# Two thirds of layer 1's modulation: from layer 0's attention to layer 1's scans

## The chip, the cores and the metric

The kernel runs on one core of one Trainium2 chip. The metric is the time of one execution on the device in microseconds (us), a median over several runs. One core has five engines that run side by side, each through its own list of instructions in order: TensorE (PE; its weight loads are shown apart as PEld), VectorE (DVE), ScalarE (ACT), GpSimd (POOL) and SyncE (SP), which here only issues the transfers between HBM and the core's memory.

## What is computed

A two-layer backbone with 512 latent and 256 context tokens of width 1024. Each layer has three mixers beside each other (RWKV-7 scans in both directions, latent attention, Hyena long convolutions), one output projection over all three, and a large feed-forward part (FFN) that picks experts. Each layer's normalisations and residual gates are set by a *modulation*, which depends on the conditioning vectors alone:

```python
mod_l = (jax.nn.silu(c) @ mod_w[li] + mod_b[li])[:, None, :]
mod_c = (jax.nn.silu(c_ctx) @ mod_w[li] + mod_b[li])[None, None, :]
shm_l, scm_l, gm_l, shf_l, scf_l, gf_l = jnp.split(mod_l, N_MOD, axis=-1)
p_l = (rms_norm(x, mix_norm[li]) * (1.0 + scm_l) + shm_l) @ w_in[li]
# ... rw_l, ml_l, hy_l: the three mixers on p_l ...
x = x + gm_l * (jnp.concatenate([rw_l, ml_l, hy_l], axis=-1) @ w_out[li])
x = x + gf_l * peer_ffn(rms_norm(x, ffn_norm[li]) * (1.0 + scf_l) + shf_l, ...)
```

`mod_w[li]` is a matrix of 1024 x 6144 in float32. Its first two sixths (`shm`, `scm`) are wanted at the layer's start, the third (`gm`) at the output projection, the fourth and fifth (`shf`, `scf`) at the FFN's norm, the last (`gf`) at the FFN's end.

## The kernel before

**The modulation.** `mods(li, ...)` computes one layer's modulation in 12 groups of 512 columns (two groups to a sixth). A group is 8 chunks of 128 rows. For a chunk SP loads a tile `w` of 256 KB (L400), ACT copies it to a rounded tile `wh` (L403), DVE, or POOL for every fourth chunk, forms the rest `wl = w - wh` (L404), and PE multiplies both with four columns of the conditioning (`silr`), two matmuls of 4x512 outputs into one PSUM tile. Behind the 8 chunks ACT copies the 4x512 sums to `row` (L408), four small matmuls with `sel` turn them, and DVE adds the bias into `modc` (L412). PSUM tiles have tags; the tag `ch`, with two buffers, is used both by these groups and by the steps of the RWKV scans (`rwkv_chain`).

**Who runs when.** The program is recorded once. `weave` takes tracks (generators) and always records the next piece of the track whose counter is lowest; a piece adds the number that it yields, which `scaled` multiplies. A track can also wait for marks (`after`). So the order on each engine is fixed by these numbers, and each engine then works through its own list.

In layer 0 the tracks are the scans, `hyenas()` (the convolutions), `attention()` and a statistic. When the scans are done, `hyenas()` goes on with `mods(1, ...)`, all 12 groups of layer 1, with 5 buffers of `w` and 3 of `wh` and `wl` (`MB = (5, 3)`) and a scale of 3.5 (`MS`). At that time `attention()` is in the latents' attention `mla(0, 1)`: per head the projection and rotation of q and k, the scores' maxima (`mx`, `top`), and a loop over blocks of keys (`tr<-qT,kTl`, the exponential `PT` on ACT L1225, `mm<-PT,Vl`), then a reciprocal (`rc`, L1231) and `zl` (L1233). The output projection `mixed(0, 1)` follows: per m one column block of the weights, 24 matmuls, the residual `row` (L762) and its squares, and at the end the norm for the FFN (`rsqrt` on DVE, a transposition at L623).

In layer 1, `scan()` does the scans over the latents, six steps of preparation and four chained sub-steps each (`rwkv_chain`: `R`, `U`, `S`), then the readout `rwkv_read` (`Y`, `zl` at L1102). `hyenas()` ends with the latents' convolution `hyena(1, 1)`, and `attention()` with `mla(1, 1)`. Nothing else is in the weave; then all pools but the layer's are closed and `mixed(1, 1)` and `ffn(1)` are recorded. The loads of `w_out` (L658) and of the residual rows (L593) come from SP's one queue.

Of the kernel before, what the change touches and what calls it, by code (L numbers as in the profile page):

```python
# [10 lines left out]
F32 = mybir.dt.float32  # L11
# [148 lines left out]
NL, NS = 12, 0.1  # L160
MB, CS, MX = (5, 3), 20, 0
FH = ()
MS, OX = 3.5, (2, 1)
HP, HC, HT = 300, 300, 300


# [78 lines left out]
class K:  # L245
# [137 lines left out]
        self.sel = sp.tile([4, 2], F32, name="sel")  # L383
        nc.vector.tensor_tensor(self.sel, self.ident[0:4, 0:2], self.ident[0:4, 2:4], op=OP.add)

    def mods(self, li, side, bufs, hb, es):

        nc, io = self.nc, self.io
        m = self.modc[li] = self.keep.tile([128, 48, 2], F32, name=f"modc{li}")
        sc = self.nrm[li] = self.keep.tile([128, 2, 8, 2], F32, name=f"sc{li}")  # L390
        mp, mw = [es.enter_context(self.pool(n, k, side=side)) for n, k in (("modp", 1), ("modw", 4))]
        b = mp.tile([128, 48], F32, name="b")
        nc.sync.dma_start(b, io["mod_b"][li])
        nr = mp.tile([128, 2, 8], F32, name="nr")
        nc.sync.dma_start(nr, io["norms"][li])
        for g in range(12):
            p = self.ps("ch")
            for k in range(8):
                w = mw.tile([128, 512], F32, name="w", bufs=bufs)
                nc.sync.dma_start(w, io["mod_w"][li, 128 * k:128 * k + 128, g * 512:(g + 1) * 512])  # L400
                wh = mw.tile([128, 512], F32R, name="wh", bufs=hb)
                wl = mw.tile([128, 512], F32R, name="wl", bufs=hb)
                nc.scalar.activation(wh, w, AF.Copy)  # L403
                (nc.gpsimd if k % 4 == 3 else nc.vector).tensor_tensor(wl, w, wh.bitcast(F32), op=OP.subtract)  # L404
                self.mm(p[0:4], self.sil[:, k], wh, k == 0, False)
                self.mm(p[0:4], self.sil[:, k], wl, False, k == 7)
            row = mp.tile([4, 512], F32, name="row", bufs=2)
            nc.scalar.activation(row, p[0:4], AF.Copy)  # L408
            p = self.ps("ch")
            for k in range(4):  # L410
                self.mm(p[:, 2 * k:2 * k + 2], row[:, k * 128:(k + 1) * 128], self.sel)
            nc.vector.tensor_tensor(m[:, 4 * g:4 * g + 4], p[:, 0:8].rearrange("p (m b) -> p m b", b=2),  # L412
                                    b[:, 4 * g:4 * g + 4, None].to_broadcast([128, 4, 2]), op=OP.add)
            if g in (3, 9):
                f = g // 6
                q = 8 * (3 * f + 1)
                nc.vector.scalar_tensor_tensor(sc[:, f], m[:, q:q + 8, :], 1.0,
                                               nr[:, f, :, None].to_broadcast([128, 8, 2]), op0=OP.add, op1=OP.mult)
            self.mark(("mod", li, g))
            yield 4  # L420
# [63 lines left out]
    def layer0(self):  # L484
        with ExitStack() as lay, ExitStack() as es:
# [17 lines left out]
            def hyenas():  # L503
                yield from self.hyena_filters(0, 0, "left")
                yield from self.hyena(0, 0, zc, "left")
                yield self.after(*FH)
                yield from self.hyena_filters(0, 1, "left")
                yield self.after("xc")
                yield from self.hyena(0, 1, zl, "left")
                yield self.after(("rwkv", 0, 1))  # L510
                es.close()
                yield from self.scaled(self.mods(1, "left", *MB, fin), MS)

            def attention():
                yield from self.mla(0, 0, [zc[:, m] for m in range(17, 21)], ymc, "right")
# [24 lines left out]
    def layer1(self):  # L540
        if self.done:
            return
        with ExitStack() as lay, ExitStack() as es:
            zl = self.open_layer(1, lay, 2)
            zkv = self.lp.tile([128, 2, TC], F32, name="zkv")
            yml = [zl[:, 11], zl[:, 15], zl[:, 12]]
            ctx = ExitStack()
            z = {}

            def scan():  # L550
# [7 lines left out]
            def hyenas():  # L558
                yield from self.hyena_filters(1, 1, "left")
                self.mark("flt")  # L560
                yield self.after("rw1")
                yield from self.hyena(1, 1, zl, "left")

            def attention():
                self.wcut = 4
                yield from self.project(1, 1, [(m, zl[:, m]) for m in ORDER], "right", self.h1)
                self.wcut = 8
                self.scale_par()
                self.mark("pl1")
                yield self.after("xc1", "flt")  # L570
                self.open_rwkv(es)
                zc = z["c"] = ctx.enter_context(self.pool("zc")).tile([128, 7, TC], F32, name="zc")
                self.rwk = [ctx.enter_context(self.pool(n, k)) for n, k in (("rwk", 1), ("rwp", 2))]
                self.mark("rwc")
                yield from self.project(1, 0, [(m, zc[:, m - 3] if m < 10 else zkv[:, m - 19]) for m in ORDER if m in (3, 4, 5, 6, 7, 8, 9, 19, 20)], "right")
                yield from self.mla(1, 0, [None, None, zkv[:, 0], zkv[:, 1]], None, "right")
                yield from self.mla(1, 1, [zl[:, m] for m in range(17, 21)], yml, "right")

            self.weave((0, self.context_out()), (0, attention()), (0, scan()), (0, self.scaled(hyenas(), HL1)))
            es.close()  # L580
            self.open_late(1)
            self.flat(self.mixed(1, 1, [zl[:, 0], zl[:, 1], zl[:, 2], *yml, zl[:, 13], zl[:, 14]], "left"))
# [1220 lines left out]
```

## Time and profile before

| what | us |
|---|---|
| median of 3 runs | 5449.75 |
| lowest, highest | 5433.88, 5454.05 |
| the profiled execution's own time | 5464.84 |
| its span on the core | 5463.1 |
| PE busy within it | 4928.4 |
| DVE busy within it | 3849.6 |

The profiled execution is one run; its span is what the trace covers, and its own time is 1.7 us longer. Busy times of PE come from recorded matmuls, which overlap their neighbours: a matmul of 512 columns is shown with 0.39 us and the next one starts 0.23 us later when the granted clock is 1.00. "Idle before, releaser" in a row names the wait of that engine just ahead of an instruction and what ended it. The layer-1 modulation lies at 998 to 1269 us, layer 1's convolution, scans and latent attention at about 3550 to 4061 us, and layer 1's output projection from 4061 to 4118 us.

### The profile page before, as it was taken

To read this page: it belongs to the slowest core of one execution; us is meant where nothing else is said; L and a number is where in the kernel's file an instruction comes from. 1 tells how busy PE (TensorE), PEld (TensorE's weight loads), DVE (VectorE), ACT (ScalarE), POOL (GpSimd) and SP (SyncE) were. 2 spreads that over 40 slices of the span, in tenths; PEclk is the share of its full clock that TensorE was granted. 3 is DMA by queue.
4 is the path that set the end of the run, shared out by engine and by line. 5 is a ranking of instruction groups with operands and counts; after the bars stand their busy time and mean duration, and the time that the engine had idled before them with its cause. 6 is when DMAs were issued, how large, how long until landed. Compare 5 with 4: busy or idle time off the path is not lost. (4 is left out here: it accounts for less than half of the span.)

```text
span 5463.1 us, 76042 instructions
## 1 busy us (share of the span) xinstructions
PE 4928.4 (90%) x28693; PEld 3745.5 (69%) x28693; DVE 3849.6 (70%) x8277; ACT 1918.5 (35%) x3438; POOL 1241.3 (23%) x933
## 2 busy tenths in 40 slices
PE   7987998889989999999999678888889889999998
PEld 4765676547644588887878456656657667888887
DVE  6356666656896488887888875656646985777776
ACT  5322222443254333333333232222223454444442
POOL 2322212221200122222222363211122321111110
PEclk9977899899999999999999889777899999999999
DMA  6300121342365788888888764200022668888885
GB/s 207 103 22 31 51 86 55 113 151 71 109 187 162 240 326 316 330 323 311 318 325 303 274 238 153 77 1 1 1 74 82 196 191 295 324 322 312 321 320 206
DMA packets 395517, 1028.18 MB, mean 188 GB/s; under 512 B 31780, under 2 KB 198981, under 8 KB 339597
## 3 DMA queue, kind: packets, MB, share of 16 engines
q1 hardware_dynamic: 339852, 620.65, 34.0%
q0 software_dynamic: 55296, 402.68, 19.6%
q8 instruction: 225, 3.69, 0.3%
q14 instruction: 144, 1.17, 0.1%
HBM read 920.19 MB, written 103.02 MB: 187 GB/s over the span
## 5 line engine op out<-in xcount | busy, mean ns | idle before, releaser
L203 POOL DMA_INDIRECT row<-in_uv,idx x384 | 531.8, 1385 | 1860.8 <-DVE acc L241 1586.7
L659 ACT ACTIVATE wh<-w 128x1024 fp32r<-128x1024 f32 (+1 forms) x557 | 571.0, 1027 | 1049.5 <-PE mm L272 461.7
L272 PE MATMUL mm<-hlo,wh 128*128 128x512 f32 (+2 forms) x2408 | 877.0, 368 | 30.7 <-DVE zl L688 7.5
L272 PE MATMUL mm<-hhi,wh 128*128 128x512 f32 (+2 forms) x2408 | 866.8, 364 | 0.0
L660 DVE TENSOR_TENSOR wl<-w,wh 128x1024 fp32r<-128x1024 f32 x424 | 516.3, 1221 | 255.0 <-ACT wh L659 252.1
L272 PE MATMUL mm<-hhi,wl 128*128 128x512 f32 (+2 forms) x2408 | 531.5, 361 | 1.7 <-POOL wl L660 1.7
L272 PEld LDWEIGHTS mm<-hlo,wh 128*128 128x128 f32 x2408 | 461.2, 192 | 104.4 <-issue 18.4
L241 DVE SCALAR_TENSOR_TENSOR acc<-row,act,acc 128x1024 f32<-128x1024 f32 x381 | 496.5, 1303 | 35.3 <-ACT act L237 34.6
L272 PEld LDWEIGHTS mm<-hhi,wh 128*128 128x128 f32 x2408 | 461.5, 192 | 61.8 <-issue 3.3
L219 DVE SCALAR_TENSOR_TENSOR row<-row,xk 128x1024 f32<-128x1024 f32 x384 | 480.3, 1251 | 16.5 <-DMA row<-in_uv,idx 16.3
L272 PE MATMUL mm<-row,wh 128*128 128x512 f32 (+1 forms) x1056 | 455.5, 574 | 29.9 <-DMA wh<-in_uT 25.1
L272 PEld LDWEIGHTS mm<-hhi,wl 128*128 128x128 f32 x2408 | 425.9, 189 | 56.6 <-issue 3.8
L660 POOL TENSOR_TENSOR wl<-w,wh 128x1024 fp32r<-128x1024 f32 (+1 forms) x133 | 291.4, 2198 | 670.0 <-ACT wh L659 405.3
L272 PEld LDWEIGHTS mm<-row,wh 128*128 128x128 f32 x1056 | 195.3, 195 | 211.2 <-issue 165.4
L236 ACT ACTIVATE act<-act 128x1 f32<-128x1 f32 x384 | 75.7, 197 | 498.6 <-DVE row L219 498.3
L1779 ACT ACTIVATE stage<-ch 128x512 f32<-128x512 f32 x224 | 218.2, 1101 | 62.6 <-PE ch L272 59.8
L1546 ACT ACTIVATE g<-mm 128x512 f32<-128x512 f32 (+1 forms) x256 | 137.6, 538 | 232.3 <-PE mm L272 197.2
L272 PE MATMUL rw<-wh,cl 128*128 128x512 f32 x512 | 201.5, 394 | 6.5 <-DVE cl L1614 3.5
L272 PE MATMUL rw<-wl,ch 128*128 128x512 f32 x512 | 200.5, 392 | 0.0
L272 PE MATMUL rw<-wh,ch 128*128 128x512 f32 x512 | 199.9, 390 | 0.0
L272 PE MATMUL ch<-wh,cl 128*128 128x512 f32 x512 | 199.6, 390 | 0.0
L272 PE MATMUL ch<-wh,ch 128*128 128x512 f32 x512 | 199.4, 389 | 0.0
(542 smaller groups left out, 10206.0 us busy)
## 6 DMA issues: line engine op xcount, KB each, us to landing
w<-in_uv SPq DMA_DIRECT2D x256, 512.0 KB
w<-in_uT SPq DMA_DIRECT2D x190, 512.0 KB
Wd<-stage SPq DMA_DIRECT2D x28, 2048.0 KB
w<-in_mod_w SPq DMA_DIRECT2D x192, 256.0 KB
wh<-in_uT SPq DMA_DIRECT2D x66, 512.0 KB
W<-Wd SPq DMA_DIRECT2D x32, 1024.0 KB
W<-Wd SPq DMA_DIRECT2D x32, 768.0 KB
w<-in_wq SPq DMA_DIRECT2D x32, 512.0 KB
```

The costliest lines, as they stand in the source:

```text
L203: self.nc.gpsimd.indirect_dma_start(out=row, out_offset=None, in_=self.k.io[f"uv{self.li}"], in_offset=bass.IndirectOffsetOnAxis(ap=self.t ...
L219: nc.vector.scalar_tensor_tensor(row[:, 0:1024], row[:, 0:1024], 1.0, self.x, op0=OP.mult, op1=OP.mult, accum_out=act)
L236: nc.scalar.activation(act, act, AF.Gelu)
L241: nc.vector.scalar_tensor_tensor(self.acc, row[:, 1024:], act, self.acc, op0=OP.mult, op1=OP.add)
L272: self.nc.tensor.matmul(out, lhsT, rhs, start=start, stop=stop, skip_group_check=True)
L659: self.nc.scalar.activation(wh[:, s], w, AF.Copy)
L660: eng.tensor_tensor(wl[:, s], w, wh[:, s].bitcast(F32), op=OP.subtract)
L1546: nc.scalar.activation(g, p[:, 0:ND], AF.Gelu)
L1779: nc.scalar.activation(stage[:, :, u:u + 4].rearrange("p a t -> p t a"), p, AF.Copy, scale=1 / GS)
```

## The change

`mods` takes the groups that it is to do. In layer 0's `hyenas()` it now does groups 0 to 3 (`shm`, `scm`), with buffers and scale as before. Groups 4 to 11 (`gm`, `shf`, `scf`, `gf`) are done at the end of layer 1's `hyenas()`, behind the latents' convolution, with 3 buffers of `w`, 2 of `wh` and `wl`, and a scale of 8 (`ML1`). The pools of the second call are closed behind the weave of layer 1. The bias and the norms' weights are loaded a second time.

```diff
-MS, OX = 3.5, (2, 1)
+MS, ML1, OX = 3.5, 8.0, (2, 1)
...
-    def mods(self, li, side, bufs, hb, es):
+    def mods(self, li, side, bufs, hb, es, groups=range(12)):
...
-        m = self.modc[li] = self.keep.tile([128, 48, 2], F32, name=f"modc{li}")
-        sc = self.nrm[li] = self.keep.tile([128, 2, 8, 2], F32, name=f"sc{li}")
+        if groups[0] == 0:
+            self.modc[li] = self.keep.tile([128, 48, 2], F32, name=f"modc{li}")
+            self.nrm[li] = self.keep.tile([128, 2, 8, 2], F32, name=f"sc{li}")
+        m, sc = self.modc[li], self.nrm[li]
...
-        for g in range(12):
+        for g in groups:
...
-                yield from self.scaled(self.mods(1, "left", *MB, fin), MS)
+                yield from self.scaled(self.mods(1, "left", *MB, fin, range(4)), MS)
...
-            ctx = ExitStack()
+            ctx, fin = ExitStack(), ExitStack()
...
                 yield self.after("rw1")
                 yield from self.hyena(1, 1, zl, "left")
+                yield from self.scaled(self.mods(1, "left", 3, 2, fin, range(4, 12)), ML1)
...
             self.weave((0, self.context_out()), (0, attention()), (0, scan()), (0, self.scaled(hyenas(), HL1)))
+            fin.close()
             es.close()
```

The order of instructions shows where the moved pieces come to stand. On PE at the end of layer 0's output projection, before (group 11 has the PSUM tile `ch_11321`, `tr` are the norm's sums, L623 is the norm's transposition):

```order
L272 MATMUL ch_11285<-sel_109,row_11283 128x2 x4
L272 MATMUL ch_11321<-wh_11324,silr_106 4x512
L272 MATMUL tr_10708<-sq_11215,ones_80 2x512
L272 MATMUL ch_11321<-wl_11325,silr_106 4x512
L272 MATMUL ch_11321<-wh_11332,silr_106 4x512
L272 MATMUL ch_11321<-wl_11333,silr_106 4x512
L272 MATMUL ch_11321<-wh_11340,silr_106 4x512
L272 MATMUL tr_11293<-ones_80,sq_11291 128x2 x4
```

and the same place now (L627 is the line that was L623):

```order
L272 MATMUL mm_10749<-mhi_10471,wh_10744 128x512
L272 MATMUL mm_10749<-mhi_10471,wl_10743 128x512 x8
L272 MATMUL tr_10489<-sq_10776,ones_80 2x512
L272 MATMUL tr_10781<-ones_80,sq_10779 128x2 x4
L627 MATMUL tr_10801<-ident_69,rsy_10788 128x128 x4
```

The rest of group 10 and all of group 11 stood between the last output matmul and the norm's transposition; now nothing does. Everywhere else in layer 0's attention, too, PE's list is the same with the matmuls of groups 4 to 11 taken out.

On PE at the last scan step of layer 1, before (`Y` is the readout's transposition, `top` the last head's maxima):

```order
L777 MATMUL rw_33035<-ident_69,Y_31970 64x64
L272 MATMUL rw_33035<-eye_74,Y_31970 64x64
L272 MATMUL tr_33617<-ident_69,top_33615 1x128 x4
L272 MATMUL tr_33624<-qT_33366,kTl_33364 128x512
L272 MATMUL mm_33623<-PT_33626,Vl_32134 128x512
```

and now, with a group's matmuls ahead of a chained sub-step (`ch_32517` is group 7, `ch_32590` the third of the four sub-steps):

```order
L272 MATMUL ch_32517<-wl_32569,silr_106 4x512
L272 MATMUL ch_32517<-wh_32576,silr_106 4x512
L272 MATMUL ch_32517<-wl_32577,silr_106 4x512
L272 MATMUL mm_33537<-kTl_33228,qT_33230 128x512
L272 MATMUL ch_32584<-sel_109,row_32582 128x2 x4
L272 MATMUL ch_32590<-Vt_31522,FG_31621 64x64 x4
L272 MATMUL ch_32590<-S_25199,KR_31604 64x64 x4
```

Groups 4 and 5 stand at the fifth of the six steps, group 6 in the preparation of the sixth, group 7 here between its sub-steps. Group 8 stands in the last head's loop over keys, group 9 behind it, and groups 10 and 11 within the first three m of the output projection. The last head's maxima and loop now stand ahead of the readout's transpositions.

On SP around the first load of `w_out`, now (chunks of groups 9 to 11 are the `in_mod_w` rows):

```order
L402 DMA w_33195<-in_mod_w 128x512
L662 DMA w_33720<-in_w_out 128x1024
L402 DMA w_33203<-in_mod_w 128x512
L402 DMA w_33442<-in_mod_w 128x512
L402 DMA w_33450<-in_mod_w 128x512
L662 DMA w_33756<-in_w_out 128x1024
L662 DMA w_33792<-in_w_out 128x1024
L402 DMA w_33458<-in_mod_w 128x512
L402 DMA w_33466<-in_mod_w 128x512
L662 DMA w_33828<-in_w_out 128x1024
```

Before, the first four loads of `w_out` and then the residual's rows stood there in a row. Now the last chunk of group 9 and all of groups 10 and 11 stand behind the first load of `w_out`, between loads of `w_out` and of the FFN's weights `in_wq`, and the residual's rows behind all of these.

## Rows read from the trace of the kernel before

**Rows 1.** The page: busy us, share of the span and instructions of each engine.

```profile
PE 4928.4 (90%) x28693; PEld 3745.5 (69%) x28693; DVE 3849.6 (70%) x8277; ACT 1918.5 (35%) x3438; POOL 1241.3 (23%) x933
```

**Rows 2.** By stretch: length, busy us (instructions) of each engine, PEclk, DMA share, GB/s.

```profile
1085.00:1130.00 45.00, 33.71 (x127) 16.44 (x126) 29.10 (x87) 23.46 (x49) 13.56 (x11) 0.85 0.42 130
...
3550.00:3989.00 439.00, 368.07 (x3528) 265.36 (x3526) 275.26 (x771) 118.06 (x238) 56.59 (x45) 0.78 0.01 1
3989.00:4028.00 39.00, 31.64 (x327) 17.24 (x326) 21.22 (x55) 9.11 (x16) 3.73 (x3) 0.94 0.01 1
4028.00:4061.00 33.00, 25.72 (x66) 11.55 (x66) 5.33 (x4) 6.69 (x10) 4.73 (x3) 0.71 0.19 64
```

**Rows 3.** The same by stretch, of the modulation's matmuls alone (those reading `silr`).

```profile
998.00:1085.00 87.00, 25.14 (x65) 5.28 (x66) 0.00 (x0) 0.86 0.40 127
...
1130.00:1142.00 12.00, 5.28 (x16) 1.29 (x16) 0.00 (x0) 1.00 0.52 159
...
sum 271.00, PE 69.89 PEld 15.13 DVE 0.00; mean PE 17.47 PEld 3.78 DVE 0.00
```

**Rows 4.** Instructions of one chunk, 998 to 1269 us: count, then ns min/median/max.

```profile
L403 ACT ACTIVATE wh<-w x96: 612/629/634, 998.5 to 1264.5; 128x512 fp32r<-128x512 f32 x96
...
L404 DVE TENSOR_TENSOR wl<-w,wh x72: 675/686/1958, 1000.0 to 1264.4; 128x512 fp32r<-128x512 f32 x72
```

**Rows 5.** PE in time, two turns of the key loop: start, length, instruction, idle before.

```profile
1088.38 0.39 PE L272 MATMUL ch<-wl,silr 128*4 128x512 f32 x1
1088.61 1.06 PE L272 MATMUL mm<-PT,Vl 128*128 128x512 f32 x2
...
1091.28 1.06 PE L272 MATMUL mm<-PT,Vl 128*128 128x512 f32 x2
...
4053.12 1.12 PE L272 MATMUL mm<-PT,Vc 128*128 128x512 f32 x2 [0.29 <-ACT PT L1225]
...
4055.86 1.12 PE L272 MATMUL mm<-PT,Vc 128*128 128x512 f32 x2 [0.75 <-ACT PT L1225]
```

**Rows 6.** PE in time, waits in layer 0's latent attention.

```profile
1109.98 0.59 PE L272 MATMUL ch<-wl,silr 128*4 128x512 f32 x1 [3.88 <-DVE wl L404]
...
1124.55 0.59 PE L272 MATMUL ch<-wl,silr 128*4 128x512 f32 x1 [4.28 <-DVE wl L404]
```

**Rows 7.** Last residual to the norm's transposition, in time, layer 0 and then layer 1.

```profile
1256.64 0.75 DVE L762 SCALAR_TENSOR_TENSOR row<-mm,modc,row 128x512 f32<-128x512 f32 x1 [5.91 <-PE mm L272]
...
1267.61 1.05 PE L272 MATMUL ch<-sel,row 4*128 4x2 f32 x8 [0.68 <-ACT row L408]
...
1268.59 1.12 PE L623 MATMUL tr<-ident,rsy 128*128 128x128 f32 x4
...
4117.26 0.75 DVE L762 SCALAR_TENSOR_TENSOR row<-mm,modc,row 128x512 f32<-128x512 f32 x1 [5.92 <-PE mm L272]
...
4124.14 1.08 PE L623 MATMUL tr<-ident,rsy 128*128 128x128 f32 x4 [2.53 <-DVE rsy L289]
```

**Rows 8.** In time, layer 1's last chained step to the output projection.

```profile
3989.41 0.45 PE L272 MATMUL ch<-R,T 64*64 64x64 f32 x8
...
4009.19 0.68 DVE L1072 TENSOR_REDUCE st<-Y 128x8 f32<-128x512 f32 x1
...
4033.34 0.69 DVE L1102 TENSOR_TENSOR zl<-rw,g 128x512 f32<-128x512 f32 x1 [7.69 <-PE rw L272]
...
4061.24 0.76 PE L272 MATMUL mm<-mlo,wh 128*128 128x512 f32 x1 [4.26 <-DVE zl L1233]
...
4072.81 0.75 DVE L762 SCALAR_TENSOR_TENSOR row<-mm,modc,row 128x512 f32<-128x512 f32 x1 [5.23 <-PE mm L272]
```

**Rows 9.** In time: issues of `w_out`, its first split on POOL, one 256 KB load.

```profile
4034.12 14.95 SPq L658 DMA_DIRECT2D w<-in_w_out  x4
...
4044.04 4.67 POOL L660 TENSOR_TENSOR wl<-w,wh 128x1024 fp32r<-128x1024 f32 x2 [15.98 <-ACT wh L659]
...
5442.37 3.09 DMA w<-xm
```

## The prediction

> **What bounds the kernel now.** I read the busy shares first: PE is busy 4928.4 of 5463.1 us [rows 1], so a matmul that leaves a stretch where PE is full is worth its length, and one that leaves a stretch where PE waits anyway is worth nothing. So the two places were read by stretch. At the place that the work leaves, PE is busy 33.7 of 45 us in the first stretch, and much of that is the modulation itself [rows 2, 3]; its other work waits for chains through DVE and ACT [rows 5, 6]. At the place that it goes to, PE is busy 368 of 439 us during the scans, 31.6 of 39 in the last chained step and the readout, and 25.7 of 33 in the last head of attention [rows 2]. Last, the rows in time where the moved groups come to stand: the norm at the end of layer 0 [rows 7] and the way from the last scan step to the output projection [rows 8, 9].
>
> The sum is made against the profiled execution, 5464.84 us, 15 us above the median of the three runs; I carry the difference over to the median.
>
> **What layer 0 gains.** The modulation's matmuls record 69.9 us of PE from 998 to 1269 us, of which 25.1 lie before 1085, where groups 0 to 3 end and nothing changes [rows 3]. So 44.8 us of records are taken out, and eight `sel` parts of 1.05 us [rows 7]. The records overlap: matmuls start 0.23 us apart [rows 5], so the time on PE is 128 x 0.23 + 8 x 1.05 = 38 us, the upper bound of the gain at full clock. I go through the places.
>
> The key loops: two turns with modulation matmuls in them lie 2.67 us apart, two turns in layer 1 with nothing in between 2.74 us apart [rows 5]. The turn is set by scores, exponential on ACT and product; the modulation fills its holes. Taking it out gains 0.
>
> Preparing q and k of the third pair of heads: PE waits 3.88 and 4.28 us, ended by `wl` on DVE [rows 6]. DVE and POOL do the rotation and the norm in these waits, and `wl` only stands behind them, so the waits themselves remain; what goes is the DVE time of `wl` between the steps and the matmuls between the transpositions. Bounds 0 and 8.2 us, taken 3.7.
>
> The scores' maxima: 16 matmuls of the modulation with 5.28 us of records lie in 12 us [rows 3]. Spaced 0.23 us, with a `sel` group, they hold PE 4.7 us; without them the maxima on DVE come next. Bounds 0 and 4.7, taken 3.4. The last head's maxima and the start of the output projection are alike; smaller, since a reciprocal stands in the way at both: 1.3 and 2.5 us, estimates from the same spacing and from two `wl` of 0.69 us that stand ahead of a wanted split [rows 4].
>
> The norm: from the last residual to the transposition it takes 11.95 us in layer 0, with 20 matmuls of groups 10 and 11 and their `wl` between the steps of `rsqrt`, and 6.88 us in layer 1 without them [rows 7]. Gain 5.1 us, the best founded term.
>
> Together 16 us. A colder PE takes some back: the first stretch, with its long waits, shows a granted clock of 0.85 and the records of its matmuls are 0.59 us instead of 0.39 behind the waits [rows 2, 6]. I take 2 us for that. **Gain 14 us, bounds 6 and 24.**
>
> **What layer 1 pays before the last chained step.** Groups 4, 5 and 6 are 48 matmuls and three `sel` parts: 48 x 0.23 + 3 x 1.05 = 14.2 us at full clock, about 26 at a clock of one half. From 3550 to 3989 PE is idle 71 us of 439 [rows 2], so the lower bound is 0. DVE with 275 of 439 us and ACT with 118 have room for 0.69 and 0.63 us a chunk [rows 2, 4], and the loads meet a DMA share of 0.01. PE's order is fixed, though: matmuls of the modulation stand ahead of the scan's, and cover a wait only where they happen to meet one. I take half, 7 us. The recording also draws four turns of the last heads' key loops and some maxima ahead of this point, some 10 us of PE; half of it, 5 us. **12 us later, bounds 0 and 26.**
>
> **What it pays behind it.** Call the start of the last chained step T0, 3989.4. The chain takes 19.8 us to the readout's first reduction, the readout 24.1 us to its last `zl`, and PE starts on the output projection at T0 + 71.8 [rows 8]. Between `zl` and that start the last head's loop and a reciprocal remain, 27.9 us.
>
> Now group 7 stands between two chained sub-steps, and both want the `ch` buffers: its 8 chunks lie in series with the chain. By the PE time it costs 4.7 us, at the pace of loads worked out below 12; I take 8.4. The last head's loop with group 8 now goes beside the readout, on a PE that would wait. So the first `zl` comes at T0 + 8.4 + 43.9 = T0 + 52, and attention has ended with it or within 7 us: T0 + 59, 13 us earlier than before.
>
> That is given back in SP's queue. The first load of `w_out` waits for the readout's `zl` (it is issued 0.8 us behind it [rows 8, 9]), and 17 chunks of groups 9 to 11 stand behind it. With 3 buffers and a load of 3.09 us [rows 9], a copy of 0.63 and a difference of 0.69 [rows 4], a chunk takes (3.09 + 0.63 + 0.69) / 3 = 1.5 us. But between them stand further loads of `w_out`, which wait for splits: the first four took 14.95 us to issue, the second pair only when POOL had begun the first split at 4044.0 [rows 9]. Step by step from T0 + 52: chunks up to the sixth behind T0 + 64, the next ones of group 10 until T0 + 75, and PE ends m = 0 at T0 + 76, since that group's matmuls stand among those of m = 0. Only then is the split's buffer free for the fifth load of `w_out`, behind which the last three chunks and then the residual's rows wait. The chunks are done at T0 + 88, the rows, two loads of `w_out` size further, at T0 + 92, and m = 2 starts then. Before it started behind m = 1, at 4073.6 - 3989.4 = T0 + 84 [rows 8]. **8 us, bounds -13 (all of it hidden, the head's earlier end kept) and 26** (the 17 chunks at twice the pace, 17 x 1.5 more).
>
> Layer 1 pays 12 + 8 = 20 us. With 14 gained the sum is +6 us: 5471 by the profiled execution, **5455 us** by the median (5449.75 + 6). A difference of 0.5% or 27 us is about what a measurement of this kernel can tell from no change; so I call it no change.
>
> **The rivals.** *The queue decides: slower.* The mechanism is SP's order alone. If a load shares the DMA with `w_out` so that a chunk takes 3.0 us instead of 1.5, the end of group 11 comes 26 us later, PE stands in m = 1 for it, and layer 1 pays 46: net +32, 5482 us. Even with layer 0's gain, the kernel is slower than before from about 1.2 us a chunk on, by over 0.5% from about 2.7. For it: the four loads of `w_out` took 14.95 us to issue, and 96 chunks took 266 us before, 2.8 us each (the times from first to last copy [rows 4]). Against it: there PE and DVE set the pace, not the loads, and the DMA share is 0.19 in the head's stretch [rows 2].
>
> *The holes are free: faster.* PE idles 71 us during the scans and 14.6 in the 72 us from T0 to the output projection [rows 2]. If groups 4 to 6 cost nothing and the reordered end keeps its 13 us, layer 1 pays the 5 us of attention drawn ahead less 13, -8, and with 16 to 24 us from layer 0 the net is -24 to -32: 5422 us. Against it: PE's list is in order and five of eight groups stand behind T0, where 80 matmuls and five `sel` parts need 24 us.
>
> *It takes out fillers only.* If the gain at the maxima and the preparation is 0 as in the key loops, layer 0 gives the norm's 5 us less 2 and layer 1 costs what was said: net +17, 5467 us. For it: the waits of rows 6 end with DVE work that stays.
>
> *A colder layer 0.* The matmuls taken out kept PE busy in the holes of attention; the stretch with long waits has the clock at 0.85, and in the last head of layer 1, with nothing to fill in, it is 0.71 [rows 2]. If all of the attention from 1085 on, some 114 us to the output projection, ran at 0.71 instead of 0.85, and PE worked half of it on other matmuls (an estimate: it is busy three quarters of the first stretch [rows 2], a third of that with fillers), 57 us would grow by 57 x (0.85 / 0.71 - 1) = 11: the gain shrinks to 3, net +17, 5467 us. Against it, two turns without filler are 2.74 us apart, as short as filled ones [rows 5]. [...]
>
> **How the numbers follow.** The forecast 0.42, the queue 0.18, free holes 0.17, fillers only 0.14, colder 0.09. The forecast's own range, from its bounds taken half way, is 5435 to 5475, and it holds the last two rivals' times too. Below it lie most of the free holes, above it most of the queue's case; the range of 8 in 10 cuts the outer part of both: 5424 to 5486. Faster by over 0.5% (under 5422.5): half of the free holes and 0.03 of the forecast, 0.12. Slower by over 0.5% (over 5477): two thirds of the queue, a quarter of the two rivals at 5467 and 0.02, 0.20. Within: 0.68.
>
> **What would show it.** Layer 0: the norm from the last residual to the transposition takes 7 us, and the FFN starts some 14 us earlier; if 5, only fillers went. The granted clock of that attention tells the colder case. Layer 1: the last chained step shifts, beyond layer 0's gain, by 12 us, none of it if the holes are free; group 7's matmuls stand between two sub-steps with a gap of some 8 us in the chain. SP's issues of the modulation behind the first `w_out` at 1.5 us each, or 3; PE waiting for `wl` in m = 0 and m = 1, and `row` at m = 0 waiting for a DMA. I am wrong if these loads are issued ahead of `w_out`, or if the scans lose more than 26 us.

## The result: slower by 59 us

The changed kernel takes 5511.3 us (median of 4 runs, 5505.2 to 5520.3), the kernel before 5451.9 us (4 runs, 5433.9 to 5470.2). The ratio is 1.011 with an interval of 1.0084 to 1.0135. The forecast was 5455 us, a range of 5424 to 5486 and 0.20 for slower.

The two profiled executions differ by 42.7 us of span. In the one of the changed kernel everything from 470 us on, in code that is the same, already came 14 us earlier; executions of one kernel differ by such amounts (see the end). So I compare lengths between marks in the program, not times from the start. The marks are `zl` behind a head of attention, `top` (maxima), `Ktok` (the end of a scan step's preparation), the residual `row` and the norm's transposition.

| stretch, between marks | before, us | after, us | difference |
|---|---|---|---|
| layer 0: q, k and maxima of the third pair, `zl` to `top` | 36.4 | 35.6 | -0.8 |
| its two key loops, `top` to last `zl` | 53.0 | 55.7 | +2.7 |
| output projection to the last `row`, and the head ahead of the third pair | 90.8 | 96.2 | +5.4 |
| the norm, last `row` to transposition | 12.0 | 7.9 | -4.1 |
| layer 0 together | 192.2 | 195.4 | +3.2 |
| layer 1: second to sixth of its nine `Ktok` (three of the context, six of the latents), ahead of group 4 | 303.7 | 287.0 | -16.7 |
| the step with group 4 | 55.2 | 66.2 | +11.0 |
| the step with group 5 | 86.7 | 104.9 | +18.2 |
| the step with group 6 | 55.9 | 60.5 | +4.6 |
| last `Ktok` to the first residual `row` | 79.1 | 117.5 | +38.4 |
| from there to the norm | 57.3 | 55.1 | -2.2 |
| layer 1 together | 637.9 | 691.2 | +53.3 |

Together +57 us, as the runs say. The FFN between them differs by 2 us. So layer 0 gained nothing and layer 1 pays everything.

The page of the changed kernel shows next to nothing of this, where [rows 1] answer to it: the same instructions, 9 us more of PE.

```profile
PE 4937.4 (90%) x28693; PEld 3743.3 (68%) x28693; DVE 3854.6 (70%) x8277; ACT 1920.7 (35%) x3438; POOL 1248.1 (23%) x933
```

**Layer 0.** Busy time by stretch (length, PE, PEld, DVE, ACT, POOL, PEclk, DMA), first of the kernel before, the third pair's q, k and maxima and the norm:

```profile
1104.38:1140.73 36.35, 24.83 (x97) 12.33 (x96) 28.18 (x91) 17.30 (x36) 10.54 (x8) 0.81 0.43 132
...
1256.64:1268.59 11.95, 9.56 (x48) 4.21 (x46) 9.61 (x26) 9.68 (x20) 2.72 (x2) 1.00 0.33 99
```

and the same of the changed kernel:

```profile
1090.90:1126.49 35.59, 20.04 (x44) 10.88 (x44) 14.00 (x74) 6.66 (x15) 4.39 (x4) 0.56 0.00 0
...
1249.57:1257.45 7.88, 2.07 (x10) 1.08 (x11) 6.20 (x22) 6.95 (x17) 0.00 (x0) 0.87 0.15 50
```

In the first stretch 53 of 97 matmuls are gone and half of DVE's work, and it is as long as before: 44 matmuls now take 20.0 us, at a granted clock of 0.56 instead of 0.81. The rows in time show it, where [rows 6] answer to them: PE idles 6.5 us for the rotation on POOL, and then two scores of 256 columns are recorded with 1.06 us and two of 512 with 1.91. The same scores in the kernel before:

```profile
1129.50 0.60 PE L272 MATMUL mm<-kTc,qT 96*128 96x256 f32 x2
1129.93 1.02 PE L272 MATMUL mm<-kTl,qT 96*128 96x512 f32 x2
```

and in the changed kernel:

```profile
1111.64 1.09 PE L1202 MATMUL tr<-ident,x 128*96 128x128 f32 x4 [6.50 <-POOL x L1198]
1113.50 1.09 PE L1202 MATMUL tr<-ident,x 128*96 128x128 f32 x4 [0.77 <-ACT qT L1204]
1114.38 1.06 PE L272 MATMUL mm<-kTc,qT 96*128 96x256 f32 x2
1115.23 1.91 PE L272 MATMUL mm<-kTl,qT 96*128 96x512 f32 x2
```

The output projection has another reason. It takes 67.4 us instead of 62.9, and 4.1 of the 4.5 lie between its first two `row`s. The norm of the context is a track of its own, and with the eight groups gone its pieces are recorded earlier among the projection's matmuls: here PE's list is more than the old one with the groups taken out. PE now waits longer for that norm's `rsqrt` on DVE, before and then after:

```profile
1210.55 0.40 PE L623 MATMUL hy<-ident,rsy 128*128 128x128 f32 x2 [0.70 <-DVE rsy L289]
...
1200.44 0.40 PE L627 MATMUL hy<-ident,rsy 128*128 128x128 f32 x2 [3.10 <-DVE rsy L289]
```

Of the ten traces in which layer 0 has groups 0 to 3 alone, eight show a projection of 66.8 to 70.6 us, and two one of 63.5.

**Layer 1.** The steps with groups 4, 5 and 6, before and then after:

```profile
3789.92:3845.15 55.23, 53.91 (x580) 38.15 (x580) 33.76 (x76) 16.00 (x31) 5.02 (x4) 0.85 0.01 2
3845.15:3931.85 86.70, 68.17 (x626) 47.49 (x625) 55.47 (x153) 22.46 (x45) 12.47 (x10) 0.82 0.00 1
3931.85:3987.73 55.88, 49.88 (x570) 38.15 (x570) 38.38 (x105) 15.14 (x32) 7.58 (x6) 0.82 0.01 1
```

```profile
3759.89:3826.04 66.15, 63.93 (x608) 43.35 (x608) 37.55 (x82) 21.94 (x43) 7.57 (x6) 0.81 0.11 33
3826.04:3930.94 104.90, 83.69 (x654) 53.90 (x654) 64.85 (x176) 27.79 (x57) 16.24 (x13) 0.74 0.07 21
3930.94:3991.46 60.52, 57.16 (x612) 39.24 (x612) 41.37 (x101) 22.03 (x42) 9.17 (x7) 0.92 0.12 36
```

One group stands in each of these steps, between two chained sub-steps (its first matmuls start at 3796.9, 3849.0 and 3957.4 us), and not two at the fifth step as said ahead of the prediction. PE, which was to have holes for them, is busy longer in each, by 10, 15.5 and 7 us, and idle as long as before in the three together (26.8 us against 25.9). Summed over the trace's instructions, each up to the start of the next, the groups' matmuls take 17.3 us of PE, their `sel` parts 3.7, and attention 9.7 more, since 26 more of its matmuls stand here. PE waits 5.8 us ahead of the groups' matmuls and `sel` parts, and 6.4 us less ahead of the scan's. So these steps pay for work on PE; the waits for the supply (loads, copies, differences) are no more than what the groups cover. In all of layer 1 PE's idle time just ahead of matmuls that read `silr` is 24 us (us, times), 5 of it in these steps and the rest behind them:

```profile
  POOL wl L406: 13.3, 10
  DVE wl L406: 6.6, 7
  ACT wh L405: 4.2, 5
```

(The 71 and 33 us in the expectations of two runs below count such a wait twice, for PE's matmuls and for its weight loads.)

And the end, SP's queue in time: 17 chunks of `in_mod_w` between the loads of `w_out` and `in_wq`, from 4055.5 to 4099.2, 2.6 us each, and then, only behind the last of them, the residual's rows (`row<-xf`).

```profile
4054.87 0.33 SPq L662 DMA_DIRECT2D w<-in_w_out  x1
4055.47 5.35 SPq L402 DMA_DIRECT2D w<-in_mod_w  x3
...
4091.76 7.40 SPq L402 DMA_DIRECT2D w<-in_mod_w  x3
4099.20 0.42 SPq L662 DMA_DIRECT2D w<-in_w_out  x1
4099.68 0.42 SPq L662 DMA_DIRECT2D w<-in_wq  x1
4104.56 1.75 SPq L597 DMA_DIRECT2D row<-xf  x4
```

PE in time there, and the first residual on DVE:

```profile
4103.95 0.59 PE L272 MATMUL ch<-wl,silr 128*4 128x512 f32 x1 [0.38 <-POOL wl L406]
...
4108.97 1.41 DVE L766 SCALAR_TENSOR_TENSOR row<-mm,modc,row 128x512 f32<-128x512 f32 x2 [1.70 <-DMA row<-xf]
```

SP's order holds the rows until the last issue ahead of them, at 4099.7. Then SP waits 4.3 us more, and issues them 0.6 us after PE has started on the last tile of group 11. Its waits ahead of the rows' loads (us in total, times, longest) are for PE's `ch`, for `wl` and for a chunk's load:

```profile
SPq L597 <- PE ch L272: 2.0, 1, 2.0
SPq L597 <- DVE wl L406: 1.4, 1, 1.4
SPq L597 <- DMA w<-in_mod_w: 0.9, 1, 0.9
```

The residual's tiles are opened behind the close of the modulation's pools. These waits say that they stand in memory which those pools gave back, and so wait for its last reader, too. The kernel before shows the like: there the same loads wait for attention's last `zl`.

```profile
SPq L593 <- DVE zl L1233: 12.0, 1, 12.0
```

### The profile page after: what moved, and what is told of

Same layout as the page of the kernel before. It is cut to its first block, busy times and chain, and to the rows that moved or that the text cites. A ratio compares the mean times of both kernels' runs of the same rounds, so it can differ in the third digit from the quotient of the medians.

```text
span 5505.8 us, 76051 instructions
## 1 busy us (share of the span) xinstructions
PE 4937.4 (90%) x28693; PEld 3743.3 (68%) x28693; DVE 3854.6 (70%) x8277; ACT 1920.7 (35%) x3438; POOL 1248.1 (23%) x933
## 5 line engine op out<-in xcount | busy, mean ns | idle before, releaser
L272 PEld LDWEIGHTS mm<-hlo,wh 128*128 128x128 f32 x2408 | 461.2, 192 | 105.4 <-ACT wh L663 14.2
L1783 ACT ACTIVATE stage<-ch 128x512 f32<-128x512 f32 x224 | 218.0, 1101 | 60.1 <-PE ch L272 57.3
L272 PE MATMUL ch<-wl,ch 128*128 128x512 f32 x512 | 200.2, 391 | 0.0
```

Of the source, the lines that this page charges most:

```text
L272: self.nc.tensor.matmul(out, lhsT, rhs, start=start, stop=stop, skip_group_check=True)
L1783: nc.scalar.activation(stage[:, :, u:u + 4].rearrange("p a t -> p t a"), p, AF.Copy, scale=1 / GS)
```

## The experiments

Every ratio is against runs of the kernel before on the same chip; the chips differ between experiments. Lengths between marks come from the profiled execution of each run.

### Layer 0 alone

Groups 4 to 11 are left out; constants stand in their place.

```diff
-                yield from self.scaled(self.mods(1, "left", 3, 2, fin, range(4, 12)), ML1)
+            if li:
+                nc.vector.memset(self.modc[li][:, 16:48], 0.1)
+                nc.vector.memset(self.nrm[li][:, 1], 1.0)
```

> Groups 4 to 11 of layer 1's modulation are left out altogether (constants stand in their place), so that only what layer 0 gains is left. Theory A (PE gets colder without its fillers and layer 0 gains nothing; all of the loss is layer 1's): -4 to +5 us against the kernel before, and the stretch from the third pair's q and k to the output projection at a granted clock of 0.6 to 0.8. Theory B (the 14 us of the prediction are there, hidden by other differences between two executions): -14 us, 5436.

Ratio 1.0005 (0.9985 to 1.0026): no difference. Layer 0's stretch is 195.1 us long, as in the changed kernel. Taking out two thirds of a layer's modulation gives nothing; the interval leaves room for 8 us at most.

### Layer 1 alone

Layer 0 as before, and the eight groups a second time in layer 1.

```diff
-                yield from self.scaled(self.mods(1, "left", *MB, fin, range(4)), MS)
+                yield from self.scaled(self.mods(1, "left", *MB, fin), MS)
```

> Layer 0 does all twelve groups as in the kernel before, and layer 1 does groups 4 to 11 a second time where the changed kernel has them. Theory A: the whole loss, +55 to +62 us. Theory B: +70 us or more, since layer 0's 14 are no longer in it.

Ratio 1.0107 (1.0073 to 1.0142), +58 us: the whole loss. Its step lengths are the changed kernel's: 62, 105, 63 and 114 us where that had 66, 105, 60 and 118.

### Fillers without supply in layer 0

Layer 0 alone, as above, but the 128 matmuls stay.

```diff
                 yield from self.scaled(self.mods(1, "left", *MB, fin, range(4)), MS)
+                wd = fin.enter_context(self.pool("dum", 1, side="left")).tile([128, 512], F32R, name="wdum")
+                self.nc.vector.tensor_copy(wd, self.ones[:, 0:1].to_broadcast([128, 512]))
+                for g in range(4, 12):
+                    p = self.ps("ch")
+                    for k in range(8):
+                        self.mm(p[0:4], self.sil[:, k], wd, k == 0, False)
+                        self.mm(p[0:4], self.sil[:, k], wd, False, k == 7)
+                    yield 4 * MS
```

> As the run that leaves groups 4 to 11 out, but in layer 0 their matmuls stay on PE, on a constant tile: no load, no copy, no difference, no wait. Theory A (clock): the attention's granted clock comes back to 0.9 or more and the time falls below the run without fillers by 8 to 15 us, although PE does 30 us more of work. Theory B: fillers only cost; 0 to 5 us above the run without them.

Ratio 0.9977 (0.9958 to 0.9996), some 12 us less than before and 15 less than without the fillers, by the middle of the ratios. The medians without and with fillers, ten executions each on one chip, lie further apart, 5471.4 and 5443.8; layer 0's stretch is 195.1 and 180.4 us long. The stretch of q, k and maxima without fillers, and then with them:

```profile
1105.08:1140.68 35.60, 20.03 (x44) 10.85 (x44) 14.00 (x73) 6.67 (x15) 4.39 (x4) 0.56 0.00 0
```

```profile
1093.11:1121.55 28.44, 25.77 (x113) 11.75 (x111) 13.74 (x74) 6.55 (x15) 4.41 (x4) 1.00 0.00 1
```

More matmuls, a clock of 1.00 instead of 0.56, and 7.2 us less. The only difference between these two kernels is work that nobody reads. The two key loops with their maxima fall, too, from 55.7 to 47.2 us. The last filler starts at 1143.6, ahead of the second loop. That loop has 42 matmuls in both kernels, and still runs at 1.00; the changed kernel's, and then this run's:

```profile
1156.23:1182.16 25.93, 19.15 (x42) 8.10 (x42) 3.51 (x2) 4.17 (x7) 0.00 (x0) 0.76 0.00 1
```

```profile
1146.85:1168.75 21.90, 15.11 (x42) 6.47 (x42) 3.51 (x3) 4.17 (x7) 0.00 (x0) 1.00 0.00 1
```

The output projection stays long, 68.7 us, so what it lost is not a matter of the fillers.

### The fillers in the changed kernel

The same lines added to the changed kernel.

> The changed kernel with the 128 matmuls of groups 4 to 11 kept in layer 0 as well, on a constant tile, results unused. If the clock in layer 0's attention is what ate the gain there: 10 to 18 us less than the changed kernel, +42 to +50 against before. Rival (layer 0's fillers helped only while layer 1 was empty, or by chance of the order): within 5 us of the changed kernel.

Ratio 1.0107 (1.0077 to 1.0138). The trace has layer 0's gain, 177.8 us instead of 195.4, and the q and k stretch is 28.4 us again. But its layer 1 is 702 us long instead of 691 (8 us more ahead of group 4, 5 more with it), in the same order of instructions, and the median of the runs did not move against the changed kernel's ratio of 1.011. By the runs alone the rival came true, within 5 us of the changed kernel; the intervals leave room for 15 us. So the place is confirmed, and whether the whole program gets the gain is not.

### Another scale: all eight groups ahead of the last step

```diff
-MS, ML1, OX = 3.5, 8.0, (2, 1)
+MS, ML1, OX = 3.5, 2.0, (2, 1)
```

> The changed kernel with a scale of 2 instead of 8 for layer 1's groups: all eight stand ahead of the last scan step, none in its chain, none among the loads of w_out. Theory A (place decides: the chain's 17 us and the end's 20 to 30 us come from group 7 and from SP's order): 25 to 45 us less than the changed kernel, 5470 to 5485. Rival (each group costs some 8 to 11 us on a full and cold PE wherever it stands): 8 x 8 to 11 less the 16 that the first steps gained, 5500 to 5525.

Ratio 1.0065 (1.0048 to 1.0082), +35 us: 24 less than the changed kernel by the ratios. The end is as before (7.3 us from the last `zl` to the first residual, where the changed kernel has 38.3 and the kernel before 6.4). But the two steps that now hold all the groups are 68 and 125 us instead of 55 and 87: 51 us for eight groups, 6.3 each. Both theories had a part.

### Matmuls without supply in layer 1

As in layer 0: the 128 matmuls on a constant tile, where the changed kernel has its groups; the groups' values are constants. The lines that set these and make `wd` are as above and left out here.

```diff
-                yield from self.scaled(self.mods(1, "left", 3, 2, fin, range(4, 12)), ML1)
+                for g in range(4, 12):
+                    p = self.ps("ch")
+                    for k in range(8):
+                        self.mm(p[0:4], self.sil[:, k], wd, k == 0, False)
+                        self.mm(p[0:4], self.sil[:, k], wd, False, k == 7)
+                    yield 4 * ML1
```

> Groups 4 to 11 are not computed (constants stand in their place), but their 128 matmuls stand in layer 1 where the changed kernel has them, on a constant tile: no load, no copy, no difference, no sel part. Theory A (supply: PE stands idle 71 us ahead of these matmuls for wl and wh, and SP's order does the rest): -10 to +15 us against the kernel before. Rival (PE's own time, in its fixed order and at its colder clock): +30 us or more.

Ratio 1.0025 (1.0003 to 1.0048), +14 us. Against before the three steps are 5.0, 2.7 and 6.9 us longer, 14.6 for three groups, and the last step to the first residual 8.7. A dozen matmuls of attention are drawn ahead into these steps, too. So 48 matmuls, 11.0 us at 0.23 us each, cost about what PE needs for them even though PE has holes. The other 45 us of the changed kernel come with the supply, the `sel` parts and the different order of instructions; this run does not part them.

### Supply without its readers in layer 1

All loads, copies and differences are done, but the matmuls of groups 4 to 11 read a constant tile `wd` (made as in layer 0; those lines are left out here).

```diff
-                self.mm(p[0:4], self.sil[:, k], wh, k == 0, False)
-                self.mm(p[0:4], self.sil[:, k], wl, False, k == 7)
+                self.mm(p[0:4], self.sil[:, k], wd if groups[0] else wh, k == 0, False)
+                self.mm(p[0:4], self.sil[:, k], wd if groups[0] else wl, False, k == 7)
```

> The changed kernel with all loads, copies and differences of groups 4 to 11 in layer 1 in place, but their matmuls read a constant tile (so these groups' values are not the modulation's), and PE never waits for wl or wh. Theory A (PE's waits for the supply, in its fixed order, are what the changed kernel pays beyond the matmuls): near the run with matmuls alone (+14 us against before), at most +25. Rival (the copies and differences take ACT and DVE from the scan's own steps, and the loads take SP from w_out): +40 us or more, near the changed kernel's +60.

Ratio 1.0068 (1.0039 to 1.0098), +37 us: between the theories. All 64 copies and differences now run as early as their buffers allow, ahead of group 4, and the steps there are 307 us long instead of 286 with matmuls alone. So some 23 us go with them, though PE's order there differs a little, too. The other 22 or so of the changed kernel are its waits, its late end and its order; this run does not part them. From the last `zl` to the first residual it is 7.7 us, but that `zl` comes late: from the last `Ktok` to the first residual it is 99 us, where the kernel before has 79.

### Deeper buffers

```diff
-                yield from self.scaled(self.mods(1, "left", 3, 2, fin, range(4, 12)), ML1)
+                yield from self.scaled(self.mods(1, "left", 4, 3, fin, range(4, 12)), ML1)
```

> The changed kernel with 4 load buffers and 3 of each split tile in layer 1 instead of 3 and 2, the most that fits by this step. If the pace of a chunk (two split tiles, freed by PE) holds the groups: 10 to 20 us less than the changed kernel. If PE's order and SP's order hold them: within 5 us.

Ratio 1.0072 (1.0046 to 1.0098), +39 us, 20 less than the changed kernel. Groups 10 and 11 end ahead of attention's last `zl`, and now SP waits for that `zl` ahead of the residual's rows:

```profile
SPq L597 <- DVE zl L1237: 13.0, 1, 13.0
```

From it to the first residual it is 8.8 us, but that `zl` comes late: from the last `Ktok` to the first residual it is 105 us, where the changed kernel has 117.5 and the kernel before 79. The steps with groups 4 to 6 are 28 us longer than before instead of 34.

### Another queue

```diff
-                nc.sync.dma_start(w, io["mod_w"][li, 128 * k:128 * k + 128, g * 512:(g + 1) * 512])
+                (nc.gpsimd if groups[0] else nc.sync).dma_start(w, io["mod_w"][li, 128 * k:128 * k + 128, g * 512:(g + 1) * 512])
```

> The changed kernel with layer 1's loads of mod_w issued from POOL's queue instead of SP's, so that they and the loads of w_out and of the residual's rows no longer wait for each other. Theory A (SP's one queue makes the end late: in the changed kernel the residual's rows are issued 34 us behind attention's end): 20 to 28 us less than the changed kernel, 5483 to 5492, and the first residual within 15 us of the last zl. Rival (the chunk's own chain, three loads and two split tiles, sets the pace of groups 9 to 11): within 8 us of the changed kernel.

Ratio 1.0133 (1.0092 to 1.0173), +73 us: no help. SP's queue now holds no chunk, and the residual's rows on it still waited for the modulation, 12.9 us, most of it for its chunks:

```profile
SPq L597 <- DMA w<-in_mod_w: 9.6, 4, 4.3
...
SPq L597 <- PE ch L272: 1.9, 1, 1.9
SPq L597 <- DVE wl L406: 1.4, 1, 1.4
```

and the first residual came 50 us behind the last `zl`. The chunks themselves were no earlier: behind the last `Ktok` the copies `wh` of the next two groups begin at 11.4 and 39.9 us, where the changed kernel has 11.4 and 39.7. The theory that SP's order alone makes the end late fell here; what that order costs in the changed kernel is not shown.

### Differences on DVE alone

```diff
-                (nc.gpsimd if k % 4 == 3 else nc.vector).tensor_tensor(wl, w, wh.bitcast(F32), op=OP.subtract)
+                (nc.gpsimd if k % 4 == 3 and not groups[0] else nc.vector).tensor_tensor(wl, w, wh.bitcast(F32), op=OP.subtract)
```

> The changed kernel with every difference wl of layer 1's groups on DVE, none on POOL. PE stood idle 33 us for POOL's wl there. Theory A (supply waits): 5 to 15 us less than the changed kernel. Rival (DVE is what the scan's steps wait for, and 16 more differences of 0.69 us stand in its list): 0 to 10 us more.

Ratio 1.0083 (1.0053 to 1.0112), +45 us, 15 less than the changed kernel in the middle, with intervals that meet. The steps with groups 4 to 6 are 16 us longer than before instead of 34; the end is as late (43 us).

### Fewer groups in layer 1

Groups 10 and 11 go back to layer 0, then 7 to 11; the lists of groups in the two calls are all that changes.

```diff
-                yield from self.scaled(self.mods(1, "left", *MB, fin, range(4)), MS)
+                yield from self.scaled(self.mods(1, "left", *MB, fin, [0, 1, 2, 3, 10, 11]), MS)
-                yield from self.scaled(self.mods(1, "left", 3, 2, fin, range(4, 12)), ML1)
+                yield from self.scaled(self.mods(1, "left", 3, 2, fin, [4, 5, 6, 7, 8, 9]), ML1)
```

> Layer 1 does groups 4 to 9, layer 0 the others and groups 10 and 11. If the changed kernel's late end (38 us from the last zl of attention to the first residual, where before had 6) is made by groups 10 and 11, whose tiles must be read before the residual's rows can be loaded: that step is 6 to 12 us, and the time 20 to 30 us less than the changed kernel, +30 to +40 against before. If it is group 7 to 9 or the loads of w_out: within 10 us of the changed kernel.

Ratio 1.0038 (1.0011 to 1.0064), +21 us: 39 less than the changed kernel. All else in its trace is the changed kernel's to the microsecond: 286.9 us ahead of group 4, then 65.6, 105.1 and 60.5, but 82.6 from the last `Ktok` to the first residual instead of 117.5. On DVE the last `zl` and the first residual:

```profile
4077.61 0.69 DVE L1237 TENSOR_TENSOR zl<-mm,rc 64x512 f32<-64x512 f32 x1
...
4084.19 0.75 DVE L766 SCALAR_TENSOR_TENSOR row<-mm,modc,row 128x512 f32<-128x512 f32 x1 [4.49 <-DMA row<-xf]
```

So groups 10 and 11 make 35 us of the loss, and groups 7 to 9 with the reordered end 3.5.

Fewer still, groups 4 to 6 alone:

> Layer 1 does only groups 4, 5 and 6, which the changed kernel has ahead of the last chained step; layer 0 does the other nine. If the end's cost lies in groups 7 to 11, and the first steps' gain of about 15 us and the three groups' cost of 34 us (both from the changed kernel's trace) stay: +10 to +25 us against before, and from the last attention's zl to the first residual 7 us. If any group beside the scans spoils the order as much as eight do: +40 us or more.

Ratio 1.0070 (1.0043 to 1.0097), but its eight runs lie in two heaps, two at 5452 and 5456 us and six from 5483 to 5496, and the profiled execution is one of the two. In that trace layer 1 is 640.6 us long, +3 against before, with the end as before. What the six lose has no trace. With fewer groups moved than the run before it (+21 us) it is slower, so a sum over groups does not explain it; this run stays open.

Group 4 alone was to be a version that beats both:

> Layer 1 does only group 4, layer 0 the other eleven. In the changed kernel's trace the steps ahead of group 4 were 17 us shorter and group 4's own step 11 us longer than before. If both stay: -10 to 0 us against before, a version that could beat both kernels. If the shorter steps come only with more groups, or one group costs as much as three: +5 to +30 us.

Ratio 1.0018 (0.9996 to 1.0039). Its trace has layer 1 at 629 us, 9 less than before; the runs don't confirm a gain.

### Cheaper fillers in the kernel before

Three attempts at the kernel before itself. Every second difference on POOL:

```diff
-                (nc.gpsimd if k % 4 == 3 else nc.vector).tensor_tensor(wl, w, wh.bitcast(F32), op=OP.subtract)
+                (nc.gpsimd if k % (2 if li else 4) == (1 if li else 3) else nc.vector).tensor_tensor(wl, w, wh.bitcast(F32), op=OP.subtract)
```

> The kernel before, with every second difference wl of layer 1's modulation on POOL instead of every fourth. If what layer 0's fillers cost is DVE's time (the run that keeps only their matmuls was 12 us faster than before): 3 to 6 us less than before. Rival: POOL needs 1.28 us for one where DVE needs 0.69 and stands ahead of the rotation's steps, so 0 to 5 us more.

Ratio 1.0016 (0.9991 to 1.0040): no difference. The last groups ahead of the norm:

```diff
-MS, OX = 3.5, (2, 1)
+MS, OX = 2.5, (2, 1)
```

> The kernel before with a scale of 2.5 instead of 3.5: layer 0 keeps all twelve groups, but the last two stand between the output projection's matmuls instead of between the last of them and the FFN's norm. The norm's step, 12.0 us before and 7.9 in the changed kernel, gets 4 us shorter; theory A: 2 to 5 us less than before. Rival (PE is full in the output projection, so it pays there): 0 to 3 us more.

Ratio 1.0018 (0.9999 to 1.0038): the norm is 8.7 us instead of 12.0, but the output projection ahead of it pays more than that: layer 0's stretch is 201.7 us long instead of 192.2. One more matmul, on zeros, for each chunk:

```diff
+                if li:
+                    self.mm(p[0:4], self.sil[:, k], zd, False, False)
                 self.mm(p[0:4], self.sil[:, k], wl, False, k == 7)
```

> The kernel before with one more matmul for each chunk of layer 1's modulation in layer 0, on a tile of zeros, between the two that are there: more filling that waits for nothing. Theory A (the clock of the stretches with long waits is worth more than PE's time): the q and k stretch goes from a clock of 0.81 towards 1.0 and the time by -8 to 0 us. Rival (96 x 0.23 = 22 us of PE are paid where PE is full): +5 to +15 us.

Ratio 1.0019 (1.0001 to 1.0037). The clock of the q and k stretch rose from 0.81 to 0.86 only, and the stretch did not get shorter (37.7 us): PE still waits 8.5 us for `wl` there, and the step at the norm grew to 14.9 us. So fillers that stand between matmuls that wait did not help here.

## Why the prediction was wrong

**Layer 0's gain, forecast 14 us, was nothing.** The norm's term was right (4.1 us for 5.1). The first step that failed is "a colder PE takes some back: I take 2 us". For q, k and the maxima I had counted a gain of 7.1 us; without fillers the clock went to 0.56 and took it all. With fillers that wait for nothing the stretch fell by 7.9 us, to 28.4, near the 7.1. That is not the same sum, though: the fillers hold PE, and the clock rose to 1.00, where before it was 0.81. The key loops, counted as 0, became 2.7 us longer, and 5.8 shorter than before with fillers. The turns that I had held against the colder rival do stay near 2.7 us in all three kernels; the maxima and the first turn behind them do not (from `top` to the loop's second exponential, in the second loop, 9.4 us in the changed kernel, 8.0 before, 5.8 with fillers). The rival had the direction, a price of 11 us (also with the 110 us that the trace has from 1085 us to the projection, instead of 114) where the fillers gave back 15 to 18 in the traces, and a chance of 0.09; rows of layer 1's last head at 0.71 lay before me. In the changed kernel the scores behind PE's wait of 6.5 us are recorded at about twice their length (1.06 and 1.91 us, before 0.60 and 1.02). By what rule the clock is granted no run shows. The second step that failed is the start of the output projection, counted as a gain of 2.5 us: the projection became 4.5 longer, since the context's norm moved in PE's list, which I took to be the old one.

**Groups 4 to 6, forecast 12 us, cost 34 in their steps.** "I take half" of the matmuls' 14.2 us failed: they and their `sel` parts took 21 us of PE, in steps with a granted clock of 0.74 to 0.92, and what they covered of the scan's waits (6 us) was lost again in their own (6 us). The run with matmuls alone paid 14.6 for 11.0. The list is in order, and holes elsewhere in the 439 us (71 us in all in the kernel before) did not help: in these steps PE idles 26.8 us where it had 25.9. Half of the 10 us of attention drawn ahead failed as well: it was 9.7. What I counted as nothing, because DVE and ACT "have room", is PE's 6 us of waits here; the run with unread supply suggests that 64 copies and differences can cost the scan's steps some 20 us at busy shares of 63% and 27%. What I did not foresee at all is that the steps ahead of group 4 are 17 us shorter. PE's order differs there from the kernel before (pieces of attention and of the scan are exchanged). Nine traces with the changed kernel's list there have 283 to 295 us, six with before's list 297 to 305. So the gain goes with the order; what in it makes the gain is not shown, and nothing in the change aimed at it. So the two together, 17 us against a forecast of 12, come near it by luck alone.

**The end, forecast 8 us, cost 36.** The chain of steps was worked out to the right place, the residual's rows behind the modulation's last chunk, but its steps were too short. T0 is 3993.1 us here. Group 7 stood in the chain and made it 17 us longer (45.6 to 62.7 us from the last `Ktok` to the readout's `zl`) where I took 8.4, so the first load of `w_out` came at T0 + 62 instead of T0 + 52. The 17 chunks behind it took 44 us instead of 36, at 2.6 us each. And one wait was not in the prediction: the rows wait 4.3 us for the memory of the modulation's tiles, so for PE's last matmul of group 11. The third m started at T0 + 117, where I had T0 + 92:

```profile
4109.78 0.79 PE L272 MATMUL mm<-mlo,wh 128*128 128x512 f32 x1 [2.71 <-DVE row L766]
```

Attention's earlier end gave 10 to 14 back, as forecast, but behind the late rows that was worth nothing; the six-group run shows group 7's cost and this gain near even, at +3.5 us.

**The rival of the queue** had the right direction and a chance of 0.18, and its price, +32, was the sum of the forecast and chunks at 3.0 us. Three terms were too small in the same direction at once, which bounds taken one at a time did not hold: 20 us forecast for layer 1 against 53 measured.

## What to carry to other kernels

Work of an engine that stands in the holes of a waiting chain may cost nothing where it is and give nothing when it goes: ask what the granted clock would be without it before counting its removal as a gain. Here the clock went from 0.81 to 0.56 and the stretch from 36.4 to 35.6 us. Moved under another stretch, such work paid about its full length here (14.6 us for 11.0 us of matmuls), since the engine's list is in order; the mean idle share of that stretch, 71 of 439 us, said nothing on it. Look at what else moves in the lists, as the context's norm and pieces of attention did here. And look at what is placed in the moved work's memory afterwards: here the loads of the residual's rows waited 4.3 us for the last uses of the modulation's tiles.

## What was not expected of the hardware

A stretch of 44 matmuls took 35.6 us with a mean granted clock of 0.56 of full speed, and 28.4 us at 1.00 with 69 matmuls more; the key loop behind the last filler ran at 1.00 with none of its own, where the changed kernel has 0.76. And executions of one kernel differ by up to 58 us on one chip (5433 to 5491 in 15 runs of the kernel before), with parts of the program 7 to 14 us longer or shorter in the same order of instructions: the second `Ktok` of layer 0's scans at 474.4 us before and at 460.7 after, the scan steps ahead of group 4 from 297 to 305 us in six traces and from 283 to 295 in nine.
